# Weight-block sums of a Strassen-Winograd SwiGLU product moved from VectorE into accumulating DMAs

## The chip, the cores and the metric

The kernel runs on 1 core of one Trainium2 chip. The metric is device microseconds (us) of one execution, from the program's start to its end on that core. PE is TensorE, DVE VectorE, ACT ScalarE, POOL GpSimd and SP SyncE, which here issues the DMAs.

## The reference

One pre-norm layer over 1024 tokens and 1024 channels in float32: three parallel mixers (convolution, gated linear attention, differential attention), gates, an output projection, and then the channel mixer, which this case is about:

```
x = x + y @ w_out[l]
h = rms_norm(x, norm_ffn_g[l])
gate, up = jnp.split(h @ w_ffn_in[l], 2, axis=-1)
x = x + (jax.nn.silu(gate) * up) @ w_ffn_out[l]
...
return rms_norm(x, final_norm_g)
```

`w_ffn_in` is 1024 x 5632, so `h @ w_ffn_in` has 22 stretches of 256 output columns.

## The kernel before

**Exact parts.** Every operand of a matmul is held as a rounded high part and a low part, the rest. `hilo` makes them: ACT writes the high part (a CAST), then DVE subtracts it from the source. `mm3` then does three matmuls: high x high, high x low, low x high. In the rows `wh` and `wl` are the parts of a weight block.

**The SwiGLU's first product** goes in 22 units of 256 output columns, even units gate and odd units up. A unit's weights are four blocks a11, a21, a12, a22 of 128 x 512 (two halves of K, two halves of the columns). The 1024 tokens and the halves of K make the right operand 2 x 2 blocks as well, so that Winograd's form of Strassen's algorithm does with seven block products p = 0 to 6 what would be eight. Their right operands are, in the order of p, "11", T1, T2, "21", T3, T4, "22"; T1 to T4 are sums of blocks of h. In the rows `b` is "11", "21" or "22" and `bT` is T1 to T4. The left operands are a11 (p = 0), a12 (3), a22 (5) and four sums: s1 = a21 + a22 (p = 1), s2 = s1 - a11 (2), s3 = a11 - a21 (4), s4 = a12 - s2 (6). DVE makes the four sums (`comb`, L951) out of the raw weights that SP loads.

Each product is 4 x 3 = 12 matmuls of 512 columns. A unit's products 0, 2, 4, 5 add up in one half of a PSUM tile of two banks (`sc`), 1 and 6 in the other half, and 3 is alone in a bank (`pb`). In between, ACT copies what stands there (`copy`, L1008: "p1" after p = 0, "u2" after p = 2, "u3" after p = 4), and `finish` adds these copies to other products (DVE, L996), and applies silu (ACT, L1000) or the multiplication with the gate (DVE, L1003). Whether the two halves of `sc` are read and written independently is decided per tile: a product that writes one half waits for the reading of the other.

**What sets the order.** `order` is the list of products as PE does them, `makes` the list in which the left operands are made, seven products ahead (`AHEAD`). A scheduler then moves instructions of each engine within that order, for instance some matmuls of another product into a gap where one waits. There are eight buffers each for `wh` and `wl`, two for raw weights, four (`s2`) for the sums. Each engine takes its instructions in order. SP's queue holds the weight loads, the stores of the products to `m_d` and other loads; GpSimd does only small powers for the RMSNorm there (L122) and no DMA.

The blocks "11" to T4 are made by `ffn_norm` while the output projection ends and the first products run, T4 by `t4_block` in four quarters.

Of the kernel before, what the change touches and what calls it, by code (L numbers as in the profile page):

```python
# [42 lines left out]
def units():  # L43
    """Order in which the 256-column weight units are consumed."""
    out = []
    for h in range(NH):
        out += [("CV", 2 * h), ("A", h), ("V", h), ("CV", 2 * h + 1), ("OG", h)]
        if h < NH - 1:
            out += [("MG", h)]
    for j in range(ND // 2):  # L50
        out += [("DV", j), ("QK", 2 * j), ("MD", j), ("QK", 2 * j + 1)]
    out += [("MG", NH - 1)] + [("MC", u) for u in range(4)]
    out += [("PW", u) for u in range(4)]
    out += [("WO", u) for _ in range(2) for u in range(4)]
    for j in range(FT // 2):
        out += [("FG", j), ("FU", j)]
    out += [("FO", j) for j in range(FT // 2)]
    return out
# [9 lines left out]
def body(nc, tc, I, out):  # L68
# [40 lines left out]

    def hilo(hi, lo, src):  # L110
        act.copy(hi, src)  # L111
        vec.tensor_tensor(out=lo, in0=src, in1=f(hi), op=ALU.subtract)  # L112

# [5 lines left out]
    def rstd(dst, ss, n, width):  # L119
        """dst = (ss / n + eps) ** -0.5"""  # L120
        vec.tensor_scalar(out=dst, in0=ss, scalar1=1.0 / n, scalar2=EPS, op0=ALU.mult, op1=ALU.add)
        pool.tensor_tensor(out=dst, in0=dst, in1=mhalf[:, 0:width], op=ALU.pow)  # L122

    # ---- weights: stream of units, one ahead of its use, split in pieces behind the products
    ready = deque()
# [48 lines left out]

    # ---- work that runs behind the projections: generators, each yields after how many
    # parts of a projection (8 products) it goes on
    events, clock = [], {"now": 0, "seq": 0, "conv": 0.0}
# [36 lines left out]

    # ---- hidden state, transposed: [channel, token] in two exact parts
    def transposed(src, hh, hl, half, gcol):
# [43 lines left out]

    # ================= RMSNorm of x, transposed
    q4 = lambda name="q4": mix.tile([P, S + 32], F32, tag="q4", name=name, bufs=10)
# [44 lines left out]

    # ================= low-rank forget gate: rows 32 j to 32 j + 15 get h @ W_f with the
    # upper part of W_f, the next 16 rows that with its lower part
    ws = q4("ws").bitcast(F32R)  # L310
# [18 lines left out]

    # ---- lambda of the differential attention, and its norm's weights  # L330
    lq = mix.tile([P, 256], F32, tag="h2", name="lq", bufs=10)
# [13 lines left out]

    # ---- gates: sigmoid(x) = (1 + tanh(x / 2)) / 2; what a gate multiplies carries the half
    def sigmoid2(out_, x):
# [4 lines left out]

    # ================= A. convolution
    csum = q4("csum")[:, 0:S]
# [31 lines left out]

    # ================= B. gated linear attention
    e4 = lambda name: mix.tile([P, S], F32, tag="e4", name=name, bufs=2)
# [179 lines left out]

    # ================= C. differential attention
    A = {}  # L570
# [165 lines left out]

    # From here on the tokens go in two parts: tiles 0, 1, 4, 5 and tiles 2, 3, 6, 7
    PARTS = ((0, 1, 4, 5), (2, 3, 6, 7))
# [6 lines left out]

    # ================= convolution: LayerNorm over channels, swish
    def conv_norm(cs):
# [74 lines left out]
    spawn(conv_split(1))  # L822
    # ================= pointwise convolution, gate, sum of the branches
    yset = bigset(keep, "kb", "y")
# [23 lines left out]

    # ================= output projection, residual, RMSNorm
    # The SwiGLU's first product is taken in 2 x 2 blocks (output columns and tokens, halves of K)  # L850
    # by Winograd's form of Strassen's algorithm: seven block products in place of eight.
    # right operands: "11", "21", "22" (blocks of h) and T1..T4 (their sums)
    B = {}
# [7 lines left out]
    def ffn_norm(t):  # L861
        xt = x2.pop(t)
        sp.dma_start(x2_d[t], xt)
        xn = b4("xn")
        ssc, rc = sm[:, 16 + t:17 + t], sm[:, 24 + t:25 + t]
        act.activation(xn, xt, AF.Square, accum_out=ssc)
        rstd(rc, ssc, D, 1)
        vec.scalar_tensor_tensor(out=xn, in0=xt, scalar=rc, in1=ffg, op0=ALU.mult, op1=ALU.mult)
        yield 4 if t in PARTS[0] else 3 if t < 4 else 2
        tt = slice(t % 4 * P, (t % 4 + 1) * P)  # L870
        v4 = lambda a: a.rearrange("p (k c) -> p k c", k=4)
        v4f = lambda a: a.bitcast(F32)

        def put(name, src):
            hilo(B[name][0][:, :, tt], B[name][1][:, :, tt], v4(src))

        pts = []
        for g in range(2):
            pt = bank()
            for k in range(4):  # L880
                pe.transpose(pt[:, k * P:(k + 1) * P], xn[:, (4 * g + k) * P:(4 * g + k + 1) * P], ident)
            pts.append(pt)
        old = lambda name, p: f(B[name][p][:, :, tt])
        if t < 4:
            put("11", pts[0])
            yield 2 if t in PARTS[0] else 0
            put("21", pts[1])
            return
        u, v = b4("u"), b4("v")
        t1, t2_, r12, t3 = u[:, hs(0)], u[:, hs(1)], v[:, hs(0)], v[:, hs(1)]  # L890
        vec.tensor_tensor(out=v4(t1), in0=v4(pts[0]), in1=old("11", 0), op=ALU.subtract)
        vec.tensor_tensor(out=v4(t1), in0=v4(t1), in1=old("11", 1), op=ALU.subtract)
        act.copy(r12, pts[0])
        put("T1", t1)
        yield 2 if t in PARTS[0] else 0
        vec.tensor_tensor(out=t2_, in0=pts[1], in1=t1, op=ALU.subtract)
        put("T2", t2_)
        yield 2 if t in PARTS[0] else 0
        put("22", pts[1])
        vec.tensor_tensor(out=t3, in0=pts[1], in1=r12, op=ALU.subtract)  # L900
        put("T3", t3)
# [25 lines left out]
    for half in range(2):  # L927
# [3 lines left out]
        for u in range(4):  # L931
            run(out_proj(half, u))
    # ================= SwiGLU, first product
    NU = FT
# [6 lines left out]
    def lefts(n):  # L941
        if n == 1:
            a11, a21, a12, a22 = (raw1[:, i, :] for i in range(4))
        else:
            r0 = raw_half(first + n, 0)
            r1 = raw_half(first + n, 1)
            a11, a21, a12, a22 = r0[:, 0:HALF], r0[:, HALF:], r1[:, 0:HALF], r1[:, HALF:]

        def comb(name, a, b, op):
            o = s2(name)  # L950
            vec.tensor_tensor(out=o, in0=a, in1=b, op=op)  # L951
            return o

        s_ = {}
        p = None
        while True:
            p = yield operand(s_[p]) if p is not None else None
            if p in (0, 3, 5):
                s_[p] = {0: a11, 3: a12, 5: a22}[p]
            elif p == 1:  # L960
                s_[1] = comb("s1", a21, a22, ALU.add)
            elif p == 2:
                s_[2] = comb("s2", s_[1], a11, ALU.subtract)
            elif p == 4:
                s_[4] = comb("s3", a11, a21, ALU.subtract)
            else:
                s_[6] = comb("s4", a12, s_[2], ALU.subtract)

    order = [(0, 0), (0, 3), (1, 0), (1, 3), (0, 1), (1, 1), (0, 2), (1, 2), (0, 4), (1, 4), (0, 6), (1, 6), (0, 5)]
    for n in range(1, NU):  # L970
        if n + 1 < NU:
            order.append((n + 1, 0))
        order += [(n, 5), (n, 6)] if n > 1 else [(n, 5)]
        if n + 1 < NU:
            order += [(n + 1, p) for p in range(1, 5)]
    makes = list(order)
# [5 lines left out]
    def make():  # L982
        if nxt[0] < len(makes):
            n, p = makes[nxt[0]]
            nxt[0] += 1
            if n not in gens:
                gens[n] = lefts(n)
                next(gens[n])
            made[n, p] = gens[n].send(p)

    def finish(n, i, k, add=None, src=None):
        gate = n % 2 == 0
        key = (n // 2, i, k)
        if add is not None:
            t = (y2 if len(fbs) == 0 else m2 if gate else c2)("t")
            vec.tensor_tensor(out=t, in0=src, in1=add, op=ALU.add)  # L996
            src = t
# [7 lines left out]

    def copy(src):
        c = (c2 if fbs else y2)("c")
        act.copy(c, src)  # L1008
        return c
# [12 lines left out]

    # the second product's operands
    mids, x3 = {}, {}
# [23 lines left out]
    for at, (n, p) in enumerate(order):  # L1048
# [35 lines left out]
        if p == 0:  # L1084
            ch["p1"] = copy(o)
        elif p == 2:
            ch["u2"] = copy(o)
        elif p == 3:
# [4 lines left out]
        elif p == 5:  # L1093
            finish(n, 1, 0, None, o)
        elif p == 6:
            finish(n, 0, 1, ch["u2"], o)

    drain()
    fbs[0].release()

    # ================= SwiGLU, second product, residual, RMSNorm
    fc = tc.alloc_tile_pool(name="fc", bufs=1)
# [107 lines left out]
```

## Time and profile before

| what | value |
|---|---|
| median of 2 runs | 2171.72 us (2170.72 and 2172.71) |
| span of the profiled execution | 2171.2 us; its own time is one of the two runs, so at most 1.5 us lie around the span |
| PE busy | 2147.5 us, 99% |
| DVE, ACT busy | 1385.6 us (64%), 859.0 us (40%) |
| chain that ended last | PE 95%, DVE 3%, DMA 1% |
| SwiGLU's first product | from about 1493 to 1922 us of the span |
| DMA | 177.65 MB, mean 82 GB/s, all moved on hardware queues |

A matmul's busy time overlaps that of the next, so the pace of PE is read from the distance between starts. In a timeline a row gives start, duration, engine, line, operation, output and inputs with their shapes; in square brackets stand the idle time of the engine before it and what ended it.

### The profile page before, as it was taken

The page shows a single profiled execution, that of the slowest core. Times are in us where ns is not written, and L with a number is a line of the kernel's source. Part 1 is how long each engine was busy: PE and PEld are TensorE (multiplying, and loading weights), DVE is VectorE, ACT ScalarE, POOL GpSimd, SP SyncE. Part 2 cuts the span into 40 slices and gives each one's busy share as a digit, 9 for nine tenths or more (in the row PEclk, how much of TensorE's full clock was granted, in tenths as well). Part 3 has the DMA queues.
Part 4 walks back from the last instruction along what each step waited for, and adds up shares of the span by engine and source line. Part 5 has one row for each costly group of instructions (what it writes and reads, how often), then busy time and mean ns, then how long its engine had stood idle before and what let it go on. Part 6 is the DMA issues. An engine that isn't in the chain of part 4 may idle for free.

```text
span 2171.2 us, 27863 instructions
## 1 busy us (share of the span) xinstructions
PE 2147.5 (99%) x10988; PEld 1787.7 (82%) x10988; DVE 1385.6 (64%) x2088; ACT 859.0 (40%) x1729; POOL 45.5 (2%) x45
## 2 busy tenths in 40 slices
PE   8999999999999999999999999999999999999998
PEld 6988988889887878778777888898888888888886
DVE  5988798789755454454545356567755545576766
ACT  6342251342345455455545354234433333341212
POOL 0000000000000000000000000000000000000000
PEclk9999999999999999999999999999999999999999
DMA  4112112121121111110111265443322222282111
GB/s 159 39 59 68 59 41 77 49 74 55 48 78 30 49 44 40 35 59 25 59 35 53 71 241 165 131 140 122 107 89 78 92 73 81 85 292 97 59 39 78
DMA packets 65059, 177.65 MB, mean 82 GB/s; under 512 B 6720, under 2 KB 17600, under 8 KB 64928
## 3 DMA queue, kind: packets, MB, share of 16 engines
q1 hardware_dynamic: 64928, 175.88, 24.4%
q8 instruction: 86, 1.41, 0.3%
q14 instruction: 45, 0.37, 0.1%
HBM read 137.58 MB, written 38.27 MB: 81 GB/s over the span
## 4 chain that ended last, share of the span: by engine, by line
PE 95%; DVE 3%; DMA 1%; issue 0%; POOL 0%; ACT 0%; SPq 0%; DVEq 0%; POOLq 0%; ACTq 0%
PE pb L115 22%; PE pb L116 22%; PE pb L117 22%; PE sc L115 6%; PE sc L116 5%; PE sc L117 5%; PE sc L643 3%; PE pb L678 3%; PE sc L642 3%; PE pb L667 1%; POOL sm L122 0%; DVE wl L112 0%; DVE xn L1127 0%; PE pb L712 0%; PE pb L504 0%
## 5 line engine op out<-in xcount | busy, mean ns | idle before, releaser
L115 PE MATMUL pb<-h,wh 128*128 128x512 f32 x1152 | 462.8, 402 | 0.0
L117 PE MATMUL pb<-h,wl 128*128 128x512 f32 x1152 | 450.9, 391 | 0.0
L116 PE MATMUL pb<-h,wh 128*128 128x512 f32 x1152 | 450.6, 391 | 0.0
L111 ACT CAST wh<-wr 128x512 fp32r<-128x512 f32 x331 | 203.5, 622 | 394.4 <-DVE x L1119 122.1
L112 DVE TENSOR_TENSOR wl<-wr,wh 128x512 fp32r<-128x512 f32 x331 | 225.5, 688 | 165.3 <-ACT wh L111 163.4
L362 DVE SCALAR_TENSOR_TENSOR acc<-up,par,acc 128x1024 f32<-128x1024 f32 x240 | 307.1, 1280 | 2.7
L115 PEld LDWEIGHTS pb<-h,wh 128*128 128x128 f32 x1152 | 217.1, 188 | 48.3 <-issue 5.1
L117 PEld LDWEIGHTS pb<-h,wl 128*128 128x128 f32 x1152 | 216.6, 188 | 46.8
L116 PEld LDWEIGHTS pb<-h,wh 128*128 128x128 f32 x1152 | 217.0, 188 | 41.3 <-DVE h L228 0.9
L1119 DVE TENSOR_TENSOR x<-x,pb 128x512 f32<-128x512 f32 x176 | 120.0, 684 | 59.8 <-PE pb L117 59.2
L115 PE MATMUL pb<-wh,h 128*128 128x256 f32 x512 | 148.1, 289 | 0.0
L117 PE MATMUL pb<-wh,h 128*128 128x256 f32 x512 | 144.9, 283 | 0.0
L116 PE MATMUL pb<-wl,h 128*128 128x256 f32 x512 | 144.8, 283 | 0.0
L115 PE MATMUL sc<-bT,wh 128*128 128x512 f32 x352 | 137.0, 390 | 0.5 <-ACT bT L111 0.5
L116 PE MATMUL pb<-wl,mh 128*128 128x512 f32 x352 | 136.9, 389 | 0.0
L115 PE MATMUL pb<-wh,mh 128*128 128x512 f32 x352 | 136.9, 389 | 0.0
L117 PE MATMUL pb<-wh,ml 128*128 128x512 f32 x352 | 136.9, 389 | 0.0
L116 PE MATMUL sc<-bT,wh 128*128 128x512 f32 x352 | 136.8, 389 | 0.0
L117 PE MATMUL sc<-bT,wl 128*128 128x512 f32 x352 | 136.6, 389 | 0.0
L111 ACT CAST wh<-s 128x512 fp32r<-128x512 f32 x88 | 54.5, 621 | 129.5 <-PE sc L116 79.4
L115 PEld LDWEIGHTS pb<-wh,h 128*128 128x128 f32 x512 | 98.1, 192 | 1.2 <-issue 0.6
L116 PEld LDWEIGHTS pb<-wl,h 128*128 128x128 f32 x512 | 98.1, 192 | 0.3
(249 smaller groups left out, 3768.2 us busy)
## 6 DMA issues: line engine op xcount, KB each, us to landing
wr<-w_dram SPq DMA_DIRECT2D x176, 512.0 KB, 3.6
m_d<-t SPq DMA_DIRECT2D x44, 256.0 KB, 2.1
mr<-m_d SPq DMA_DIRECT2D x22, 512.0 KB, 5.5
y_d<-y SPq DMA_DIRECT2D x28, 256.0 KB, 2.0
xt<-x_dram SPq DMA_DIRECT2D x8, 512.0 KB, 5.4
c_d<-acc SPq DMA_DIRECT2D x8, 512.0 KB, 2.7
g_d<-sgc SPq DMA_DIRECT2D x16, 256.0 KB, 2.1
c<-c_d SPq DMA_DIRECT2D x8, 512.0 KB, 7.8
```

Source lines behind the costliest of these rows:

```text
L111: act.copy(hi, src)
L112: vec.tensor_tensor(out=lo, in0=src, in1=f(hi), op=ALU.subtract)
L115: pe.matmul(o, ah, bh, start=start, stop=False, skip_group_check=more)
L116: pe.matmul(o, ah, bl, start=False, stop=False, skip_group_check=more)
L117: pe.matmul(o, al, bh, start=False, stop=stop, skip_group_check=more)
L362: vec.scalar_tensor_tensor(out=acc, in0=up[:, j:j + S], scalar=w, in1=acc, op0=ALU.mult, op1=ALU.add)
L642: pe.matmul(sc[i][:, c], a["q"][i][:, t], a["k"][i][:, c], start=True, stop=False)
L643: pe.matmul(sc[i][:, c], a["q"][i][L, t], a["kl"][L, c], start=False, stop=True)
L667: pe.transpose(pt[:, i * P:(i + 1) * P], pd[:, (g0 + i) * P:(g0 + i + 1) * P], ident)
L678: pe.matmul(ov[:, 0:P], parts[k // 4][:, c], a["v"][:, k, :], start=k == 0, stop=k == nk - 1)
L1119: vec.tensor_tensor(out=xx, in0=xx, in1=o, op=ALU.add)
```

## The change

The sums no longer pass through DVE. `begin` copies a21 from DRAM into a buffer (SP), and `plus` adds another block of the weights in DRAM into the same buffer by an accumulating DMA, which GpSimd issues. A DMA can only add here, so signs move: s1 = a21 + a22, then + a11, then + a12 in the same buffer serve p = 1, 2, 6, and s3 = a21 + a11 serves p = 4. For that, the blocks "11" and "22" are stored negated (`hilo` with a sign), T1 and T3 are formed with the new signs, and the copies after p = 0 and p = 2 are negated while ACT takes them. The buffer of s1 is overwritten after each use, so each `plus` waits for the CAST and the low part that read it, and the next CAST waits for the DMA. For units from 3 on, `order` has p = 3 between 1 and 2, so that 4 follows 2.

```
-        def comb(name, a, b, op):
+        def blk(i):
+            return w_d[first + n, i // 2, :, i % 2 * HALF:(i % 2 + 1) * HALF]
+
+        def begin(name):
             o = s2(name)
-            vec.tensor_tensor(out=o, in0=a, in1=b, op=op)
+            sp.dma_start(o, blk(1))
             return o
 
-        s_ = {}
-        p = None
-        while True:
-            p = yield operand(s_[p]) if p is not None else None
-            if p in (0, 3, 5):
-                s_[p] = {0: a11, 3: a12, 5: a22}[p]
-            elif p == 1:
-                s_[1] = comb("s1", a21, a22, ALU.add)
-            elif p == 2:
-                s_[2] = comb("s2", s_[1], a11, ALU.subtract)
-            elif p == 4:
-                s_[4] = comb("s3", a11, a21, ALU.subtract)
-            else:
-                s_[6] = comb("s4", a12, s_[2], ALU.subtract)
+        def plus(o, i):
+            pool.dma_start(o, blk(i), accum_op=ALU.add)
+
+        s1, s3 = begin("s1"), begin("s3")
+        plus(s1, 3)
+        plus(s3, 0)
+        src = {0: a11, 3: a12, 5: a22, 1: s1, 2: s1, 6: s1, 4: s3}
+
+        def take(p):
+            o = operand(src[p])
+            if p in (1, 2):
+                plus(s1, (0, 2)[p - 1])
+            return o
+
+        return take
...
-            order += [(n + 1, p) for p in range(1, 5)]
+            order += [(n + 1, p) for p in ((1, 3, 2, 4) if n > 1 else (1, 2, 3, 4))]
...
-    def hilo(hi, lo, src):
-        act.copy(hi, src)
-        vec.tensor_tensor(out=lo, in0=src, in1=f(hi), op=ALU.subtract)
+    def hilo(hi, lo, src, sign=1.0):
+        if sign > 0:
+            act.copy(hi, src)
+            vec.tensor_tensor(out=lo, in0=src, in1=f(hi), op=ALU.subtract)
+        else:
+            act.activation(hi, src, AF.Copy, scale=-1.0)
+            vec.scalar_tensor_tensor(out=lo, in0=src, scalar=-1.0, in1=f(hi), op0=ALU.mult, op1=ALU.subtract)
...
-            hilo(B[name][0][:, :, tt], B[name][1][:, :, tt], v4(src))
+            hilo(B[name][0][:, :, tt], B[name][1][:, :, tt], v4(src), -1.0 if name in ("11", "22") else 1.0)
...
-        vec.tensor_tensor(out=v4(t1), in0=v4(pts[0]), in1=old("11", 0), op=ALU.subtract)
-        vec.tensor_tensor(out=v4(t1), in0=v4(t1), in1=old("11", 1), op=ALU.subtract)
+        vec.tensor_tensor(out=v4(t1), in0=v4(pts[0]), in1=old("11", 0), op=ALU.add)
+        vec.tensor_tensor(out=v4(t1), in0=v4(t1), in1=old("11", 1), op=ALU.add)
...
-        vec.tensor_tensor(out=t3, in0=pts[1], in1=r12, op=ALU.subtract)
+        vec.tensor_tensor(out=t3, in0=r12, in1=pts[1], op=ALU.subtract)
...
-            vec.tensor_tensor(out=t, in0=src, in1=add, op=ALU.add)
+            vec.tensor_tensor(out=t, in0=add, in1=src, op=op)
...
-        act.copy(c, src)
+        act.activation(c, src, AF.Copy, scale=-1.0 if neg else 1.0)
...
-            ch["p1"] = copy(o)
+            ch["p1"] = copy(o, True)
         elif p == 2:
-            ch["u2"] = copy(o)
+            ch["u2"] = copy(o, True)
...
-            finish(n, 0, 1, ch["u2"], o)
+            finish(n, 0, 1, ch["u2"], o, ALU.subtract)
```

Where instructions stand now, at three places. First PE in a unit in the middle, at the end of T2 (`bT_11902` high, `bT_11903` low); `b_11380` and `b_11381` are block "21". Before, all twelve matmuls of "21" follow, and then T3:

```order
L116 MATMUL sc<-bT_11903,wh 128x512
L117 MATMUL sc<-bT_11902,wl 128x512
L115 MATMUL pb<-b_11380,wh 128x512
L116 MATMUL pb<-b_11381,wh 128x512
L117 MATMUL pb<-b_11380,wl 128x512
```

PE at the same place of the changed kernel; `b_11378` and `b_11379` are block "11" of the next unit, `bT_11904` and `bT_11905` are T3:

```order
L120 MATMUL sc<-bT_11903,wh 128x512
L121 MATMUL sc<-bT_11902,wl 128x512
L119 MATMUL sc<-b_11378,wh 128x512 [waits DVE_49]
L120 MATMUL sc<-b_11379,wh 128x512
L121 MATMUL sc<-b_11378,wl 128x512
L119 MATMUL sc<-b_11378,wh 128x512
L120 MATMUL sc<-b_11379,wh 128x512
L119 MATMUL sc<-bT_11904,wh 128x512 [waits Activation_49]
```

T3 now stands five matmuls behind T2, 18 times in all; nine (seven of "11", two of "21") stand between T3 and T4, where twelve did.

Second ACT in such a unit, before, from the CAST of s1 on; `c_13413` is the copy u2:

```order
L111 CAST wh_13397<-s1_13395 128x512 [waits DVE_49,PE_49,Activation_49]
L1000 ACTIVATE t_13374<-t_13374 128x512 [waits DVE_49]
L111 CAST wh_13417<-s2_13415 128x512 [waits PE_49,Activation_49]
L111 CAST wh_13438<-wr_13338 128x512 [waits DMAHW7_49,PE_49,Activation_49]
L1008 COPY c_13413<-sc_13321 128x512 [waits PE_49]
L111 CAST wh_13462<-s3_13460 128x512 [waits PE_49,Activation_49]
```

ACT at the same place of the changed kernel; `c_13439` is u2, DMASW are semaphores of GpSimd's DMAs:

```order
L112 CAST wh_13401<-s1_13342 128x512 [waits DMASW6_49,PE_49,Activation_49]
L1009 ACTIVATE t_13382<-t_13382 128x512 [waits DMAHW6_49,DVE_49]
L112 CAST wh_13423<-wr_13340 128x512 [waits DMAHW6_49,PE_49,Activation_49]
L112 CAST wh_13441<-s1_13342 128x512 [waits DMASW4_49,PE_49,Activation_49]
L112 CAST wh_13464<-s3_13344 128x512 [waits DMASW7_49,PE_49,Activation_49]
L1017 ACTIVATE c_13439<-sc_13323 128x512 [waits PE_49]
```

Two CASTs of the same buffer now stand with one CAST of raw weights between them, and the CAST of s3 has moved ahead of u2.

Third ACT where the product starts, before: the CASTs that make the blocks T1 to T3 and "22" of the last two token tiles.

```order
L111 CAST bT20_11902<-u_12564 128x4x128 [waits DVE_49]
L111 CAST b220_11382<-pb_12559 128x4x128
L111 CAST bT10_11384<-u_12581 128x4x128 [waits DVE_49]
L111 CAST bT20_11902<-u_12581 128x4x128 [waits DVE_49]
L111 CAST b220_11382<-pb_12576 128x4x128 [waits PE_49]
```

ACT there in the changed kernel:

```order
L112 CAST bT20_11902<-u_12576 128x4x128 [waits DVE_49]
L115 ACTIVATE b220_11382<-pb_12571 128x4x128
L112 CAST wh_12659<-s1_12525 128x512 [waits DMASW4_49]
L112 CAST bT10_11384<-u_12593 128x4x128 [waits DVE_49]
L112 CAST bT20_11902<-u_12593 128x4x128 [waits DVE_49]
L115 ACTIVATE b220_11382<-pb_12588 128x4x128 [waits PE_49]
```

Unit 0's second CAST of s1 now stands among them.

## Rows read from the trace of the kernel before

**Rows 1.** The page, busy time, share of the span and instructions of each engine.
```profile
PE 2147.5 (99%) x10988; PEld 1787.7 (82%) x10988; DVE 1385.6 (64%) x2088; ACT 859.0 (40%) x1729; POOL 45.5 (2%) x45
```
**Rows 2.** Busy time by stretch, with instructions, granted clock, DMA share and GB/s.
```profile
1495.80:1499.30 3.50, 3.50 (x10) 2.68 (x10) 3.43 (x6) 0.73 (x2) 0.11 (x1) 0.51 0.00 0
1498.00:1534.00 36.00, 35.54 (x160) 29.16 (x159) 36.00 (x61) 18.96 (x34) 0.00 (x0) 0.98 0.22 74
1576.40:1614.90 38.50, 38.50 (x169) 31.38 (x168) 20.69 (x34) 13.89 (x24) 0.00 (x0) 1.00 0.26 81
```
**Rows 3.** Timeline of PE in a unit in the middle.
```profile
1666.06 0.39 PE L117 MATMUL sc<-bT,wl 128*128 128x512 f32 x1
...
1671.50 0.39 PE L117 MATMUL sc<-bT,wl 128*128 128x512 f32 x1
...
1672.64 0.39 PE L116 MATMUL sc<-bT,wh 128*128 128x512 f32 x1
1672.93 0.50 PE L115 MATMUL sc<-b,wh 128*128 128x512 f32 x1
...
1675.37 0.39 PE L116 MATMUL sc<-b,wh 128*128 128x512 f32 x1
...
1681.94 0.39 PE L117 MATMUL pb<-b,wl 128*128 128x512 f32 x1
```
**Rows 4.** Timeline of ACT in the same unit.
```profile
1671.76 0.62 ACT L111 CAST wh<-s 128x512 fp32r<-128x512 f32 x1 [1.67 <-PE sc L116]
1672.28 0.59 ACT L1000 ACTIVATE t<-sc 128x512 f32<-128x512 f32 x1
1675.84 0.62 ACT L111 CAST wh<-s 128x512 fp32r<-128x512 f32 x1 [2.96 <-PE sc L116]
```
**Rows 5.** Timeline of PE where the product starts.
```profile
1493.02 0.50 PE L115 MATMUL sc<-b,wh 128*128 128x512 f32 x1 [0.89 <-ACT b L111]
1494.77 0.63 PE L881 MATMUL pb<-cst,xn 128*128 128x128 f32 x4 [1.25 <-DVE xn L868]
...
1533.45 0.73 PE L115 MATMUL sc<-bT,wh 128*128 128x512 f32 x2 [0.46 <-ACT bT L111]
```
**Rows 6.** Groups of instructions: busy us and mean ns, idle time before, releaser.
```profile
L1008 ACT COPY c<-sc 128x512 f32<-128x512 f32 x66 | 38.3, 580 | 10.9 <-PE sc L117 10.9
L951 DVE TENSOR_TENSOR s<-wr 128x512 f32<-128x512 f32 x42 | 28.9, 688 | 22.3 <-DMA wr<-w_dram 22.3
L122 POOL TENSOR_TENSOR sm<-sm,mhalf 128x1 f32<-128x1 f32 x24 | 13.7, 569 | 894.4 <-DVE sm L121 894.4
L228 DVE SCALAR_TENSOR_TENSOR h<-pb,par,h 128x512 fp32r<-128x512 f32 x12 | 8.4, 745 | 3.1 <-ACT h L227 3.0
```
**Rows 7.** Timeline of DVE in the unit of rows 3.
```profile
1667.57 0.68 DVE L996 TENSOR_TENSOR t<-sc,c 128x512 f32<-128x512 f32 x1
...
1676.59 0.68 DVE L996 TENSOR_TENSOR t<-sc,c 128x512 f32<-128x512 f32 x1
1677.19 0.68 DVE L112 TENSOR_TENSOR wl<-s,wh 128x512 fp32r<-128x512 f32 x1
```
**Rows 8.** The page, DMA issues: count, KB each, median us to landing.
```profile
wr<-w_dram SPq DMA_DIRECT2D x176, 512.0 KB, 3.6
m_d<-t SPq DMA_DIRECT2D x44, 256.0 KB, 2.1
...
c<-c_d SPq DMA_DIRECT2D x8, 512.0 KB, 7.8
```
**Rows 9.** Timeline of DVE where the product starts.
```profile
1499.55 0.68 DVE L112 TENSOR_TENSOR wl<-s,wh 128x512 fp32r<-128x512 f32 x1
...
1533.86 0.69 DVE L112 TENSOR_TENSOR bT<-u,bT 128x512 fp32r<-128x512 f32 x1
```
**Rows 10.** Timeline of ACT there.
```profile
1503.27 0.62 ACT L111 CAST bT<-u 128x512 fp32r<-128x512 f32 x1
```

More of the change, by code (lines that the diff above doesn't have):

```diff
@@ L987, in make, with finish @@
                 gens[n] = lefts(n)
-                next(gens[n])
-            made[n, p] = gens[n].send(p)
-    def finish(n, i, k, add=None, src=None):
+            made[n, p] = gens[n](p)
+    def finish(n, i, k, add=None, src=None, op=ALU.add):
         gate = n % 2 == 0
@@ L1004, in finish, with copy @@
             sp.dma_start(m_d[2 * (n // 2) + i, :, hs(k)], t)
-    def copy(src):
+    def copy(src, neg=False):
         c = (c2 if fbs else y2)("c")
-        act.copy(c, src)
+        act.activation(c, src, AF.Copy, scale=-1.0 if neg else 1.0)
         return c
```

## The prediction, made before the changed kernel ran

> **What bounds the kernel now.** I read the busy shares first, then the windows of the SwiGLU product, then the timelines of PE, ACT and DVE inside one unit, and last the stretch in which the product starts. PE is busy for 99% of the span [rows 1], in the SwiGLU product at the full clock [rows 2]. The page warns that a busy PE may be slow, so I counted starts: from one matmul of product 22 to another 29 places later it is 1681.94 - 1675.37 = 6.57 us, 0.2266 us each [rows 3]. A unit has 84 matmuls, so 19.03 us at that pace; two units take 38.5 us, 19.25 each [rows 2]. Only some 0.2 us a unit is PE's waiting. It lies at one place: product 22 may start only when ACT has emptied what T4 left in the same tile. T4's last matmul starts at 1671.50, five matmuls of the next T1 stand in between, the fifth at 1672.64, and 22 starts at 1672.93 where 1672.87 was due; the one after it is late again [rows 3]. The reason is a short row on ACT: a CAST that T4's eleventh matmul lets go runs first (1671.76), then the eviction, 1672.28 to 1672.87 [rows 4]. DVE, whose sums the change removes, is busy 20.7 of 38.5 us [rows 2], so in the steady units a lighter DVE buys nothing.
>
> One stretch is different: from 1498 to 1534 DVE is busy all 36.00 us, 61 instructions or 0.59 us each [rows 2], and PE waits 0.46 us for the T4 block at 1533.45, after waits of 0.89 and 1.25 us as the product starts [rows 5]. All that the change could win is these 2.6 us and the 0.2 of each of 22 units: about 7 us, 0.3%.
>
> **What goes and comes.** 88 sums leave DVE (0.69 us each [rows 6]), 61 us, all but about 4 us of it in the cover just named. 132 transfers of 256 KB come, six a unit, 44 from SP and 88 from GpSimd: 1.5 MB a unit beside the 1 MB of weights and the 0.5 MB of `m_d`. DMA engines are busy 0.26 of these units [rows 2], so this makes about 0.5 and should not saturate. The scaled copies replace COPY, 580 ns, by ACTIVATE, 0.59 us out of PSUM [rows 4, 6], and the eight negated low parts take the form of 745 ns instead of one of 688 [rows 6]: 0.01 us a copy, and 8 x 0.06 in the start. I take 0.5 us for both together.
>
> **T3 behind the copy of T2.** The new order of products puts T3 behind T2 with five matmuls of the next unit's 11 in between, where twelve of 21 stood. T3 goes into the tile that u2's copy reads, and ACT runs the CAST for s3, freed by T2's eleventh matmul, ahead of that copy. This is to the instruction the pattern of 22 behind T4, so it costs the same: 0.2 us. The pattern stands 18 times: 3.6 us (1.3 to 5, from the first matmul's lateness alone, 0.07, to 0.28 with a slower tail).
>
> **T4 behind T3.** Nine matmuls now cover what twelve did. T3's last matmul starts at 1666.06, so T4 would be due at 1666.06 + 10 x 0.2266 = 1668.33; DVE's sum that it waits for ran 1667.57 to 1668.25 [rows 3, 7]. It just fits: 0 us, up to 0.1 x 18 = 2.
>
> **The wait that matters: sum behind sum.** s1 is one buffer. The CAST and the low part for T1 read it, then GpSimd adds a block, then the CAST for T2 may read it. ACT stands in order, and behind that CAST come the CAST for s3 and u2's copy, for which PE waits. So I ask how long the accumulating transfer may take, L, from the end of the low part on DVE until ACT can start. Take the unit that begins at 1671.73. The CAST for T1 starts at 1675.84 [rows 4]. DVE must first do the add that waits for 22's last matmul (1675.60 + 0.39, so about 1676.03), then the low part, 1676.63 to 1677.3; before, it stood at 1677.19 [rows 7] behind four sums and the add. By count of matmuls T2's eleventh now starts where 1681.94 stands and ends 0.39 later [rows 3]; 0.09 us on, at 1682.42, the CAST for s3 should start. The CAST for T2 must go 0.52 us ahead of it (the spacing in [rows 4]), at 1681.90. So L may be 1681.90 - 1677.3 = 4.6 us for nothing; each further us delays u2's copy, and T3, by a us, in all 18 units. The sum of s1's third block has four products' time, 10.9 us, and the two first sums are issued a unit ahead, so these are covered unless L is above 9 us.
>
> No row shows L, since no GpSimd queue moves data in the trace. From below: a 256 KB store lands 2.1 us after its issue. From above: 512 KB loads that come in a burst take 7.8. An accumulating transfer reads two 256 KB blocks and writes one, as much data in as a 512 KB load, which takes 3.6 us [rows 8]. I take 3.6, plus 0.6 for GpSimd to issue it (its shortest instruction takes 0.57 [rows 6]), plus 0.6 since the sum into the next unit's s3 is queued on GpSimd right ahead: L = 4.8, nearest to the row for equal bytes. That is 0.2 us over, 3.6 us in 18 units. With 2.1 it is nothing; with 7.8 it is 3.2 x 18 = 58 us.
>
> The Trainium skill (DMA: Bandwidth & Descriptors, Anatomy of one DMA — SWDGE (gpsimd) path) fits a GpSimd-issued DMA by 2.0 us plus bytes over 436 GB/s, an estimate of 2.6 us here. By that L would be covered, and the whole sum about +4 us. No row here shows such a transfer.
>
> **The queues.** On GpSimd the first four sums, for units 0 and 1, stand ahead of the eight small power instructions of the last RMSNorm, which PE's transposes wait for. These sums need only buffers that the pointwise stage has long freed, so I cost them at nothing; were they late, the norms and the whole start would wait. On SP the 44 first copies stand among weights and `m_d` stores and wait for a buffer's last CAST; the weights behind them are wanted a unit later, and a late copy would show as a late s3. Both are part of L's upper side.
>
> **The start.** Here ACT and DVE run without slack and four such sums stand in their order. DVE's order from the low part of unit 0's T1 (1499.55) to the last of T4's block (1533.86 [rows 9]) has 52 instructions where it had 58: 3.6 us less. Against that, with L = 4.8:
> - unit 0's second block is released at 1500.2 and lands at 1505.0. ACT would take its CAST where the trace has the CAST for T1's block, 1503.27 [rows 10]: 1.8 us lost, and DVE waits for that block.
> - unit 1's is released at about 1512.2; its CAST ends at 1517.7 and DVE, done at 1514.0, waits 3.7.
> - unit 1's third block follows at 1518.4, lands 1523.2, and DVE waits 1.9.
> - unit 2's second block is released at 1530.5 and stands ahead of the CAST for T4's third quarter: 1.9.
>
> That is 9.3 - 3.6 = 5.7 us later for T4's block; PE waited 0.46 there and two matmuls of 21 are put in between, so I take +5 us. Below L = 3.5 the waits vanish and up to 0.5 us is won. Each us of L above costs about 4. After PE idles around 1493 the clock stood at 0.51 in 1495.8 to 1499.3, the lower level [rows 2], with some 1.6 us lost; a 5 us wait could bring that again, which I keep for the upper bound.
>
> **Sum** at L = 4.8: 3.6 + 0 + 3.6 + 5 + 0.5 = 12.7 us on the span of 2171.2, which lies inside the two runs shown (2170.72 and 2172.71, median 2171.72). So 2184 us, 0.6% slower; a few tenths of a per cent are what this kernel's runs scatter by, and 2% (43 us) is what I count as a change.
>
> **Rivals.**
> - *The sums are hidden.* L at most 3.5 us: T3's 3.6 us are left and the start is even, 2176 us. For it: `m_d` stores land in 2.1 us, and the DMA engines are three quarters idle. Against it: two reads, GpSimd's own issue, and a queue of four sums a unit. The skill's fit above would give this.
> - *The sums become the bound.* The place is T2's CAST on ACT in every unit. Loss = 3.6 + 0.5 + 18 (L - 4.6) + 4 (L - 3.5); it passes 43 us at L = 6.2. At L = 7 it is 61 us, 2233 us. For it: loads in a burst take up to 7.8 us, and transfers and GpSimd's issues can only add to the row of 3.6. Against it: the units are no burst, and 3.6 us is steady for the weights there.
> - *A gain.* DVE's 61 us come off some wait of PE. Against it the count above: less than 8 us of PE's time is waiting. It could show only as 2165 us or so, never as 2%.
>
> **How the numbers follow.** My forecast, L between 3.5 and 6.2, gets 0.53; hidden sums 0.25; sums that bind 0.20; a gain 0.02. All but the third lie within 2%, so faster by over 2% is 0.01, slower 0.20, and the rest 0.79. For 8 in 10 the range goes from hidden sums, 2174, up to L = 6.5: 3.6 + 0.5 + 34 + 12 = 50 us, 2222.
>
> **What would show it.** In the profile after: GpSimd's transfers with their time to landing; L over 4.6 shows as idle ACT time ahead of the CAST for T2, ended by a DMA, and as PE waiting at T3 once a unit; units of 19.4 to 19.7 us instead of 19.25; a PE wait of some 5 us at the T4 block. I am wrong if units last over 21 us (L far longer, or SP's first copies late and GpSimd's queue stuck behind them), or if PE waits at other products than T3, 22 and T4's block.

## The result and the profile after

The changed kernel takes 2244.10 us (2 runs, 2241.17 and 2247.03) against 2171.72: a ratio of 1.0334, interval 1.0312 to 1.0355. The forecast was 2184, the range ended at 2222. The profiled execution has a span of 2239.4 us, 68.2 more than before.

The page's first line and four stretches of the windows (start:end, us, then busy time and instructions of PE, PEld, DVE, ACT and POOL, then PE's granted clock, DMA share and GB/s):

```profile
PE 2168.8 (97%) x10988; PEld 1793.4 (80%) x10988; DVE 1333.2 (60%) x2000; ACT 856.1 (38%) x1729; POOL 123.0 (5%) x133
```

```profile
1550.00:1970.00 420.00, 380.71 (x1576) 300.63 (x1575) 147.56 (x224) 128.37 (x226) 64.87 (x74) 0.96 0.59 141
1541.20:1546.80 5.60, 5.51 (x13) 4.16 (x14) 5.50 (x9) 2.12 (x5) 0.86 (x1) 0.50 0.16 30
1697.40:1701.30 3.90, 3.77 (x10) 3.02 (x11) 0.30 (x1) 0.07 (x1) 0.55 (x1) 0.57 0.63 131
1742.70:1746.60 3.90, 3.88 (x17) 3.23 (x18) 0.56 (x2) 1.01 (x2) 0.43 (x1) 1.00 0.64 131
```

DVE lost its 88 sums and nothing came of it [rows 1, 2]. PE, busy without a gap in the units of before [rows 2], is idle 39 of 420 us, and in some stretches its clock stands at the lower level: 10 matmuls in 3.9 us where 17 fit at the full clock. The waits of 1550 to 1960 us (engine and line, what it waited for, us in all, times, longest):

```profile
PE sc L119 <- ACT c L1017: 38.4, 18, 3.9
ACT wh L112 <- DMA s<-w_dram: 105.0, 18, 7.4
```

PE waits 18 times, always at T3 for ACT's copy, and ACT 18 times for a sum: the place that the forecast named. The waits come long and short by turns. A long one, all engines (start, duration, engine, line, operation):

```profile
1683.86 0.33 SPq L960 DMA_DIRECT2D s<-w_dram  x1
...
1686.16 0.62 ACT L112 CAST wh<-s 128x512 fp32r<-128x512 f32 x1 [3.18 <-PE sc L120]
...
1686.94 0.69 DVE L113 TENSOR_TENSOR wl<-s,wh 128x512 fp32r<-128x512 f32 x1
...
1688.78 1.76 POOL L964 DMA_DIRECT2D s<-w_dram  x2 [8.06 <-DVE t L1012]
...
1695.32 0.62 ACT L112 CAST wh<-s 128x512 fp32r<-128x512 f32 x1 [6.77 <-DMA s<-w_dram]
...
1696.38 0.60 ACT L112 CAST wh<-s 128x512 fp32r<-128x512 f32 x1
1696.89 0.59 ACT L1017 ACTIVATE c<-sc 128x512 f32<-128x512 f32 x1
...
1697.53 0.80 PE L119 MATMUL sc<-bT,wh 128*128 128x512 f32 x1 [3.29 <-ACT c L1017]
...
1698.12 0.63 PE L120 MATMUL sc<-bT,wh 128*128 128x512 f32 x1
1698.55 0.63 PE L121 MATMUL sc<-bT,wl 128*128 128x512 f32 x1
```

Read it downwards: CAST for T1's sum, its low part (ends 1687.63), two sums issued by GpSimd, CAST for T2's sum at 1695.32, then CAST for s3, u2's copy, and T3. L, from low part to CAST, is 7.7 us. GpSimd's first issue of the pair is for an s3 (it goes where only s3's sum is taken away, below); the one that T2 needs is the second, issued at about 1688.78 + 0.88 = 1689.66, 5.7 us ahead of the CAST. The pair itself started 1.15 us after the low part. Its first issue waits for SP's copy of 1683.86, which lands at 1688.11 by the trace's landing times, 0.67 us ahead of the pair; the row names DVE's L1012, which had ended 0.54 us earlier. From 1560 to 1960 us every sum into such a copy stands 0.66 or 0.67 us behind the landing of that copy, in the short units too, so the copy is what releases it. Behind the wait the starts are 0.43 us apart instead of 0.2266. A short one:

```profile
1665.87 0.62 ACT L112 CAST wh<-s 128x512 fp32r<-128x512 f32 x1 [2.93 <-issue]
...
1666.71 0.69 DVE L113 TENSOR_TENSOR wl<-s,wh 128x512 fp32r<-128x512 f32 x1
...
1666.93 1.76 POOL L964 DMA_DIRECT2D s<-w_dram  x2 [8.37 <-DVE t L1005]
...
1672.91 1.14 ACT L112 CAST wh<-s 128x512 fp32r<-128x512 f32 x2 [4.84 <-DMA s<-w_dram]
...
1674.60 0.50 PE L119 MATMUL sc<-bT,wh 128*128 128x512 f32 x1 [0.88 <-ACT c L1017]
1674.94 0.40 PE L120 MATMUL sc<-bT,wh 128*128 128x512 f32 x1
```

Here the pair's first issue began before the low part ended (1667.40) and was over 0.4 us behind it, and L is 5.5 us. In both units L less PE's wait is the same, 4.4 and 4.6 us: the 4.6 that the forecast had free. The page's DMA rows (queue: packets, MB, share of 16 engines' span; then count, KB each, median us to landing), with `m_d`'s stores at 3.8 where they took 2.1 [rows 8]:

```profile
q0 software_dynamic: 12672, 23.07, 6.5%
...
s<-w_dram POOLq DMA_DIRECT2D x88, 256.0 KB, 5.1
s<-w_dram SPq DMA_DIRECT2D x44, 256.0 KB, 3.9
m_d<-t SPq DMA_DIRECT2D x44, 256.0 KB, 3.8
```

The start (low part, two issues, CAST, and T4's block, for which PE waited 0.46 us before [rows 5]):

```profile
1528.97 0.69 DVE L113 TENSOR_TENSOR wl<-s,wh 128x512 fp32r<-128x512 f32 x1
...
1530.20 1.78 POOL L964 DMA_DIRECT2D s<-w_dram  x2 [4.93 <-DVE wl L113]
...
1539.58 0.62 ACT L112 CAST wh<-s 128x512 fp32r<-128x512 f32 x1 [10.58 <-DMA s<-w_dram]
...
1541.29 0.79 PE L119 MATMUL sc<-bT,wh 128*128 128x512 f32 x1 [6.28 <-ACT bT L112]
```

Here too the CAST needs the second of the pair, and the first stands 0.67 us behind the landing of a copy of SP's. The second starts at 1530.83 and lands at 1539.56, 8.7 us later; the DMA engines were 0.90 busy from 1520 to 1540 us.

**The account.** I added up, over PE's timeline, what each distance of two starts has beyond 0.2266 us, in both kernels. T3's waits: 42.4 us (the 18 above, from start to start, and one of 1.0 in the last unit). Starts at half clock behind seven of the eight longest of them in the units: 13.1. Waits of the start, from 1480 to 1560: 14.2 against 3.1, so 11.1 more, and 1.3 more in its short gaps and half clock. Small gaps at T3: 2.6. Other waits gone: -1.4. Sum 69.1, where the spans differ by 68.2.

### The profile page after: what moved, and what is told of

It reads as the page before. It is cut to its first block, busy times and chain, and to the rows that moved or that the text cites. A ratio compares the mean times of both kernels' runs of the same rounds, so it can differ in the third digit from the quotient of the medians.

```text
span 2239.4 us, 28096 instructions
## 1 busy us (share of the span) xinstructions
PE 2168.8 (97%) x10988; PEld 1793.4 (80%) x10988; DVE 1333.2 (60%) x2000; ACT 856.1 (38%) x1729; POOL 123.0 (5%) x133
## 5 line engine op out<-in xcount | busy, mean ns | idle before, releaser
L119 PE MATMUL sc<-bT,wh 128*128 128x512 f32 x352 | 147.6, 420 | 49.0 <-ACT c L1017 42.0
L120 PE MATMUL sc<-bT,wh 128*128 128x512 f32 x352 | 142.7, 406 | 0.0
L121 PE MATMUL sc<-bT,wl 128*128 128x512 f32 x352 | 142.5, 406 | 0.1
L119 PEld LDWEIGHTS sc<-bT,wh 128*128 128x128 f32 x352 | 69.5, 197 | 76.5 <-ACT c L1017 51.2
L113 DVE TENSOR_TENSOR wl<-s,wh 128x512 fp32r<-128x512 f32 x88 | 59.7, 689 | 104.7 <-ACT wh L112 104.7
```

Of the source, the lines that this page charges most:

```text
L119: pe.matmul(o, ah, bh, start=start, stop=False, skip_group_check=more)
L120: pe.matmul(o, ah, bl, start=False, stop=False, skip_group_check=more)
L121: pe.matmul(o, al, bh, start=False, stop=stop, skip_group_check=more)
```

## The experiments

The theory: what costs is the chain from CAST to CAST, by L, and the clock behind the long waits. Rival 1: the traffic, by the number of accumulating DMAs. Rival 2: the place of T3 in the new order. Ratios are to the kernel before, run on the same chip (2171.3 to 2171.7 us).

**Second and third sum on DVE.**

```
-            o = operand(src[p])
-            if p in (1, 2):
-                plus(s1, (0, 2)[p - 1])
-            return o
+            if p in (2, 6):
+                vec.tensor_tensor(out=s1, in0=s1, in1={2: a11, 6: a12}[p], op=ALU.add)
+            return operand(src[p])
```

> Of the 88 accumulating DMAs 44 stay, the first sums of s1 and s3; the second and third sum into s1 go back to DVE, so no CAST waits for a DMA that itself waits for a CAST. Theory (the chain CAST of T1's sum, low part, DMA, CAST of T2's sum takes 5.5 and 7.7 us by turns in the changed kernel, where 4.6 are free): the 42 us of waits at T3 and the stretches at half clock behind them go; what stays is 0.2 us a unit at T3 and part of the start, 2175 to 2184 us. Rival 1 (the traffic: accumulating DMAs slow the loads, and the loss goes with their number): half of the 72 us stays, about 2207 us. Rival 2 (the new order puts T3 too close behind T2's copy): T3 still waits 1 to 3 us a unit, 2230 us or more.

2175.07 us, 1.0015 (1.0005 to 1.0024). The window of the units:

```profile
1550.00:1930.00 380.00, 380.00 (x1636) 302.56 (x1635) 179.72 (x278) 137.41 (x237) 29.59 (x34) 1.00 0.50 141
```

PE has no wait at T3 left and the full clock, and the 44 DMAs that stay land in 4.0 us by the median. Rival 2 falls, and 44 such DMAs by themselves cost little, with the DMA engines 0.50 busy.

**The other half: first sums on DVE.**

```
-        s1, s3 = begin("s1"), begin("s3")
-        plus(s1, 3)
-        plus(s3, 0)
+        s1, s3 = s2("s1"), s2("s3")
...
+            if p in (1, 4):
+                vec.tensor_tensor(out={1: s1, 4: s3}[p], in0=a21, in1={1: a22, 4: a11}[p], op=ALU.add)
```

> The other half: the first sums of s1 and s3 go back to DVE, the second and third sum into s1 stay accumulating DMAs. 44 of them, as many as where only the first sums were DMAs (2175 us), but now all of them behind a CAST, and alone in GpSimd's queue. Theory (chain): L is GpSimd's start of 0.4 us and a landing of some 4.3, so 4.7 to 5 us against 4.6 free, less up to 0.5 for DVE's sums ahead of the low part: T3 waits 0.3 to 1 us in every unit alike, nothing at half clock in the units, a start of 5 to 10 us: 2185 to 2202 us. Rival (traffic by number of accumulating DMAs): 2175 us, as there. Rival (queue does not matter): 3 and 1 us by turns stay, over 2220 us.

2197.82 us, 1.0118 (1.0100 to 1.0137). The page's DMA row, the window of the units, and the wait of PE at T3 from 1550 to 1960 us:

```profile
s<-w_dram POOLq DMA_DIRECT2D x44, 256.0 KB, 4.0
```

```profile
1550.00:1930.00 380.00, 368.65 (x1578) 291.76 (x1577) 173.77 (x265) 130.58 (x230) 33.54 (x38) 1.00 0.42 108
```

```profile
PE sc L119 <- ACT c L1017: 9.2, 11, 1.5
```

As many accumulating DMAs as in the run before, the same landing and, without SP's copies, less traffic (0.42 against 0.50), but 23 us more: it matters which sums they are, not how many. Alone in GpSimd's queue the chain costs 9.2 us instead of 38.4, and no wait at T3 is followed by half clock. Most of the rest is the start (waits of 11.1 us from 1480 to 1560, against 3.1, two of them followed by half clock) and T3's place. I had expected the waits in every unit alike; but for two units early and late they stand in every second one, 0.6 to 1.5 us, where ACT has a silu (L1009, 0.5 us) between T2's CAST and s3's, and the landing is longer (4.5 against 3.9 us around 1640). Two things changed here at once: the queue is gone, and the landing fell from 5.1 us to 4.0.

**Only s3 on DVE.**

```
-        s1, s3 = begin("s1"), begin("s3")
+        s1, s3 = begin("s1"), s2("s3")
...
-        plus(s3, 0)
...
+            if p == 4:
+                vec.tensor_tensor(out=s3, in0=a11, in1=a21, op=ALU.add)
```

> Only s3's sum goes back to DVE; s1 keeps its chain of three accumulating DMAs. Theory with the queue as a part of it (in every second unit the sum that T2 needs stands on GpSimd behind the first sum of another s3, which waits for SP's copy): the waits of 3.3 us at T3 fall to the 1 us of the other units, no stretch at half clock is left, 18 x 1.1 us and a start of 5 to 10 us: 2195 to 2205 us. Theory with the landing alone (the queue does not matter): waits of 3 and 1 us by turns stay, 2235 us. Rival 1 (traffic by number of DMAs): 66 of 88 stay, about 2225 us.

2219.00 us, 1.0216 (1.0199 to 1.0233): between what the two theories said. The waits at T3, from 1550 to 1960 us:

```profile
PE sc L119 <- ACT c L1018: 25.2, 16, 5.4
```

They still come by turns, 1.5 and 0.6 us around 1690, and three of them (5.4, 3.4 and 2.2 us) are followed by half clock, which I had expected to be gone. GpSimd issues the sum 0.4 us after the low part, so the queue is gone; but in the long units DVE's other work now stands ahead of the low part, which starts 0.95 us after its CAST (1683.50 + 0.62 to 1685.07) where it took 0.16. What I expected missed that second row. The queue is a part of the loss, not all of it; this run does not size it, since the landing fell to 4.7 us by the median too.

**No adding.** The GpSimd DMAs copy; the left operands of p = 1, 2, 4, 6 are single blocks, not sums.

```
-            pool.dma_start(o, blk(i), accum_op=ALU.add)
+            pool.dma_start(o, blk(i))
```

> The 88 GpSimd DMAs copy instead of adding, so that the left operands of T1, T2, T3 and 22's second use are single blocks and not sums; order, queues and waits stay. If the adding itself makes the landing long (4.6 to 6 us from issue), it falls to 2.5 to 3.5 us, the T3 waits shrink to at most 1 us by turns, and the time to about 2190 to 2200 us. If it is the way through GpSimd, landing and time stay, about 2240 us.

2192.03 us (one run; before 2171.56). Queue, landing, and the wait at T3:

```profile
q0 software_dynamic: 7040, 23.07, 3.4%
```

```profile
s<-w_dram POOLq DMA_DIRECT2D x88, 256.0 KB, 3.2
```

```profile
PE sc L119 <- ACT c L1017: 7.5, 9, 2.5
```

The same 88 transfers of the same size from the same queue: 80 packets each instead of 144, half the engines' time, GpSimd busy 0.54 us with one instead of 0.88, landing 3.2 us instead of 5.1. So it is the adding, with the traffic that it brings, that makes the landing long, not the way through GpSimd alone.

**T1's operand made earlier.**

```
     makes = list(order)
+    for n in range(3, NU):
+        at = makes.index((n, 1))
+        makes.insert(at - 3, makes.pop(at))
```

> All DMAs stay as in the changed kernel; only the list in which left operands are made has T1's three places earlier for units from 3 on, so that low part and accumulating DMA come up to 8 us ahead of T2's CAST. Theory: the chain fits, T3 waits 0.2 us a unit, and the start's 12 us stay: 2182 to 2195 us. Rival 1 (traffic) and rival 2 (place of T3): no change, 2240 us. A third outcome, above 2240, would say that eight buffers for the operands no longer do.

2188.87 us, 1.0078 (1.0063 to 1.0093). T3's wait on the copy is gone as a PE row, though all 132 DMAs are still there, the 88 sums now land in 5.9 us by the median, and the DMA engines are busier than in the changed kernel (0.65 against 0.59). Only the weight load shows the 0.3 us a unit of the place behind u2's copy:

```profile
1550.00:1930.00 380.00, 379.82 (x1636) 302.42 (x1635) 153.63 (x235) 138.87 (x240) 64.45 (x73) 1.00 0.65 164
```

```profile
PEld sc L119 <- ACT c L1020: 6.0, 19, 0.3
```

Rival 1 falls here as a cost of its own: denser traffic, slower landing, and 55 us less. What is left of it is that the landing, a part of L, is on the whole slower with more such DMAs: over all runs the medians are 4.0 to 4.5 us with 44, 4.7 with 66, 4.6 with 82 and 5.0 to 5.9 with 88. How much of L's excess that is, and how much the queue, no run separates. The 17 us that stay are the start, which is as it was (14.1 us of waits from 1480 to 1550), and T3's place.

**The start on DVE.**

```
+        if n < 3:
+            s1, s3 = s2("s1"), s2("s3")
+        else:
+            s1, s3 = begin("s1"), begin("s3")
+            plus(s1, 3)
+            plus(s3, 0)
...
+            if n < 3 and p in (1, 2, 4, 6):
+                out, x, y = {1: (s1, a21, a22), 2: (s1, s1, a11), 6: (s1, s1, a12), 4: (s3, a11, a21)}[p]
+                vec.tensor_tensor(out=out, in0=x, in1=y, op=ALU.add)
...
-            if p in (1, 2):
+            if n >= 3 and p in (1, 2):
```

> Units 0 to 2 take all sums from DVE, the units from 3 on are those of the changed kernel. Theory: the waits between 1500 and 1545 us, 10 us at 1516, 1524 and 1541, and 2 us of half clock behind the last, come from the sums of these units by DMA; they go, and the waits at T3 from unit 3 on stay: 2228 to 2234 us. Rival: the first sums of units 3 and 4, issued in that same stretch, keep the waits, or DVE, full there before, is the limit again and gives back less: 2236 us or more.

2234.05 us, 1.0292 (1.0276 to 1.0309), 10 us back. The waits at 1509 to 1541 us are gone, T4's is 0.5 again, but one of 5.7 us for a DVE result comes behind it, as the rival had it in part; the T3 waits stay (38.4 us in 17).

**The old order with DMA sums.**

```
-            order += [(n + 1, p) for p in ((1, 3, 2, 4) if n > 1 else (1, 2, 3, 4))]
+            order += [(n + 1, p) for p in (1, 2, 3, 4)]
```

> The changed kernel with product 3 back behind product 2 in all units. Theory (chain): the CAST for T2's sum is wanted one product, 2.7 us, earlier after the low part of T1's sum; 1.9 us are left for L instead of 4.6, so PE waits some 6 and 3.7 us by turns and more of it comes at half clock: 2290 to 2310 us. Rival 2 (the place of T3 in the new order costs the time): 2175 to 2190 us.

2251.11 us, 1.0369 (1.0353 to 1.0386): some 7 us slower than the changed kernel, not 50. My expectation was wrong. It took the 2.7 us off the chain and forgot what, by a count made afterwards, the old order gives: twelve matmuls of 21 instead of five behind T2 (1.6 us), and no CAST for s3 ahead of u2's copy (0.5). 2.7 - 1.6 - 0.5 = 0.6 us a unit, and the waits at T3 rose from 38.4 to 46.0 us, 0.4 a unit. One row of it bears on the queue: at the same place GpSimd's pair is released by the DMA itself, SP's copy, issued at 1686.19.

```profile
1692.69 1.76 POOL L964 DMA_DIRECT2D s<-w_dram  x2 [8.38 <-DMA s<-w_dram]
```

**The place of T3 alone.** First sums by DMA, the others on DVE (the edit of the first experiment), and the old order:

```
-            order += [(n + 1, p) for p in ((1, 3, 2, 4) if n > 1 else (1, 2, 3, 4))]
+            order += [(n + 1, p) for p in (1, 2, 3, 4)]
```

> First sums by DMA, second and third sums on DVE, and product 3 back behind product 2. Against the same kernel in the new order (2175 us) the difference is what T3's place costs: 0.2 us in 18 units by the forecast, so 2171 to 2172 us, no change against before; 2175 us would say that the place costs nothing and the DMAs themselves cost 3 us; below 2170 us, that DVE's lighter start is worth something.

2169.98 us, 0.9994 (0.9985 to 1.0004): level with before, so 44 sums less on DVE are worth nothing that shows above the scatter. Then the kernel before in the new order:

```
-            order += [(n + 1, p) for p in range(1, 5)]
+            order += [(n + 1, p) for p in ((1, 3, 2, 4) if n > 1 else (1, 2, 3, 4))]
```

> The kernel before, all sums on DVE, with product 3 between 1 and 2 for units from 3 on and nothing else. The two runs with first sums by DMA differ by 5.1 us between the orders (2175.07 and 2169.98), 0.28 us a unit. If that is the place of T3 behind T2's copy, as the forecast has it, it shows here without any DMA: 2174 to 2178 us. If it needs the DMAs (a late CAST on ACT that T3's copy stands behind), no change: 2171 us.

2175.55 us, 1.0020 (1.0011 to 1.0029). The place costs 3.9 us without a DMA sum (2175.55 - 2171.65) and 5.1 with first sums by DMA (2175.07 - 2169.98).

**Waits without DMA sums.** The kernel before; in eight even units ACT repeats u2's copy.

```
             ch["u2"] = copy(o)
+            if n % 2 == 0 and 4 <= n < 20:
+                for _ in range(15):
+                    act.copy(ch["u2"], o)
```

> The kernel before, no DMA sums; in eight even units ACT takes the copy of T2 sixteen times over, so that PE waits for it at T3, some 2 to 4 us each. Theory (the clock falls after a wait of about 3 us of PE, whatever the cause): the waits of 3 us and more are followed by starts 0.43 us apart for some 4 us, 2 us lost for each, as in the changed kernel; 2171 + 8 x (3 + 2) = 2211 us. Rival (it is the accumulating DMAs that bring the clock down): the waits alone, 2195 us, and all starts 0.23 us apart behind them.

2234.34 us (one run). PE's timeline in one of these units, and the windows row of its slow stretch:

```profile
1639.87 0.79 PE L115 MATMUL sc<-bT,wh 128*128 128x512 f32 x1 [4.13 <-ACT c L1090]
1640.46 0.63 PE L116 MATMUL sc<-bT,wh 128*128 128x512 f32 x1
1640.88 0.63 PE L117 MATMUL sc<-bT,wl 128*128 128x512 f32 x1
...
1646.54 0.50 PE L115 MATMUL sc<-bT,wh 128*128 128x512 f32 x1 [1.45 <-ACT c L1008]
1646.88 0.39 PE L116 MATMUL sc<-bT,wh 128*128 128x512 f32 x1
```

```profile
1639.80:1645.00 5.20, 5.13 (x12) 3.80 (x12) 1.99 (x3) 0.12 (x2) 0.00 (x0) 0.53 0.25 71
```

The clock stands at its lower level behind the wait of 4.13 us and not behind that of 1.45, with no accumulating DMA in the kernel. All eight long waits (3.7 to 4.1 us) are followed by it, so a wait is enough to bring it, without these transfers. The time is 23 us above what I expected: the waits are longer than the 3 us that I had put, and the second wait, 1.2 to 1.45 us some 6 us later in each of these units, was not in my sum.

**All three taken away,** sums from unit 3 on by DMA alone:

```
+            if n < 3 and p in (2, 6):
+                vec.tensor_tensor(out=s1, in0=s1, in1={2: a11, 6: a12}[p], op=ALU.add)
...
-            if p in (1, 2):
+            if n >= 3 and p in (1, 2):
...
-            order += [(n + 1, p) for p in ((1, 3, 2, 4) if n > 1 else (1, 2, 3, 4))]
+            order += [(n + 1, p) for p in (1, 2, 3, 4)]
...
+    for n in range(3, NU):
+        at = makes.index((n, 1))
+        makes.insert(at - 3, makes.pop(at))
```

> All three causes taken away, with the sums of the units from 3 on still made by accumulating DMAs alone: T1's operand made three places earlier, product 3 back behind product 2, and in units 0 to 2 only the first sums by DMA. Theory: nothing of the loss is left, 2169 to 2173 us, no change against before. Anything over 2178 us says that a cause is missing from the account.

2171.55 us, 0.9997 (0.9988 to 1.0006).

```profile
1550.00:1930.00 380.00, 378.40 (x1651) 308.12 (x1650) 160.54 (x245) 142.53 (x245) 62.47 (x72) 1.00 0.68 170
```

With 82 accumulating DMAs in it, and the DMA engines busier than in the changed kernel (0.68 against 0.59), the loss is gone but for one wait of 1.5 us at T3: no further cause shows above the scatter. No version beats the kernel before.

## Why the prediction was wrong, step by step

- **What bounds the kernel: right.** PE does, and DVE's lighter load buys nothing: two versions with fewer sums on DVE, one without the chain and one with more time for it, stand at 0.9994 and 0.9997.
- **T3 behind u2's copy: right.** 3.6 us forecast, 3.9 and 5.1 measured. **T4:** no PE wait appears there in the units, as forecast.
- **Sum behind sum: the place and the free 4.6 us were right, L was mis-sized.** This is the step that failed. I took 3.6 us for the transfer (the row for equal bytes, 512 KB), 0.6 for the issue and 0.6 for the queue, 4.8 in all. Measured: 5.1 to 5.7 us from the issue to the CAST, and ahead of the issue 0.4 us in the short units and 2.0 in the long ones, where the sum in front waits for SP's copy and then takes 0.88 to issue. L is 5.5 and 7.7 by turns. The prediction's own formula with these two gives 9 x (0.9 + 3.1) = 36 us; T3's waits are 38.4. Counting bytes read was the wrong likeness: a copy of the same size on the same queue lands in 3.2 us, the sum in 5.1, with 144 packets for 80.
- **The queues: under-rated.** SP's copy ahead of GpSimd's sum was put down as an upper side of L; it is one of the things that made L long. The signs of being wrong had it: units over 21 us, with SP's copies late and GpSimd's queue behind them. The units lasted 22.6 us in the mean ((1945.58 - 1561.32) / 17, from T3 to T3). That the first sums ahead of the last norm's powers cost nothing was right: PE waits 1.24 us for its transposes there, 1.25 before.
- **The clock: left out of the units.** It stood in the sum's upper bound for the start only. Seven long waits cost another 13 us at the lower level.
- **The start: the mechanism right, the size twice too small.** 5 us forecast, some 12 measured: there L was 9.9 us (low part ended at 1529.66, CAST at 1539.58), where I had one L for all places. The DMA engines, 0.90 busy around it, are the likely reason; no run shows it by itself.
- **The rivals.** "The sums become the bound" came true, with 0.20. It put the 2% at L = 6.2, and the mean of the measured L is 6.6; its formula gives 3.6 + 0.5 + 18 x 2.0 + 4 x 3.1 = 53 us, and the clock about the remaining 15. By the Trainium skill's fit (DMA: Bandwidth & Descriptors, Anatomy of one DMA — SWDGE (gpsimd) path) the estimate was 2.6 us for a landing; the copy's 3.2 comes near it, the accumulating DMA's 5.1 does not, and that measurement decides.

## What to carry to other kernels

Work taken off an engine with slack was worth nothing here, and the in-place chain that replaced it (read, DMA into the same buffer, read) put a DMA's whole latency into ACT's order of work: ask how long it may take before asking how long it takes, and where the margin is tenths of a microsecond, give the chain more distance first. Here three places earlier in the list of operands were worth 55 us. A wait on the engine that bounds the kernel also has to be costed with the clock behind it.

## What the runs showed of the hardware

- An accumulating 256 KB DMA from GpSimd takes 144 packets, about twice the DMA engines' time of a plain one (6.5% against 3.4% of the span for 88), 0.88 us of GpSimd instead of 0.54, and lands in 4.0 us by the median (44 of them) to 5.9 us (88, the DMA engines 0.65 busy) instead of 3.2. In the start, with the engines 0.90 busy, single ones took up to 9.1 us.
- Behind PE's waits of 3.29 and 4.13 us the granted clock was 0.57 and 0.53 for about ten matmuls; behind 1.45 us starts kept the full pace, and behind the 2.87 us ahead of 1742.72 the clock was 1.00. The length of that one wait does not decide it: in the changed kernel starts 0.43 us apart followed a shorter wait,

```profile
1878.24 0.79 PE L119 MATMUL sc<-bT,wh 128*128 128x512 f32 x1 [2.82 <-ACT c L1017]
1878.82 0.63 PE L120 MATMUL sc<-bT,wh 128*128 128x512 f32 x1
```

and in the run with only s3 on DVE the clock was 0.63 behind a wait of 2.17 us and 1.00 behind one of 2.43. All waits of 3.0 to 6.4 us in the runs' first product were followed by the lower level.
